# A two-layer encoder trunk on one core: the norm's last squares summed in PSUM, products pinned behind the norm, state tables in fewer transfers

## The chip, the cores and the metric

The kernel runs on one core of one Trainium2 chip. The time is the device time of one execution in microseconds (us); lower is better. The engines are named as in the profile: PE (matrix products), DVE (vector), ACT (scalar), POOL (GpSimd) and SP, whose queue issues nearly all transfers.

## The reference

512 tokens of 1024 features go through two layers, float32 throughout. `u` of the input projection feeds a state-space mixer, `q`, `k`, `v` a windowed attention.

```
for i in range(2):
    x = x + 0.5 * swiglu(rms_norm(x, ffn1_norm[i]), w_gate, w_up, w_down)
    h = rms_norm(x, mix_norm[i])
    q, k, v, u = split(h @ w_in[i])
    attn = banded_attention(q, k, v, sink, bias)
    ssm = s5_mixer(u, ...)
    x = x + concat(rms_norm(attn), rms_norm(ssm)) @ w_out[i]
    x = x + 0.5 * swiglu(rms_norm(x, ffn2_norm[i]), w_gate, w_up, w_down)
return rms_norm(x, final_norm)

rms_norm: x * rsqrt(mean(x*x) + eps) * g
swiglu:   (silu(x @ w_gate) * (x @ w_up)) @ w_down
```

## The kernel before

`x` is kept transposed in SBUF: eight tiles (k0 to k7) of 128 features x 512 tokens. Every product is made of three matmuls of 128x512 (`mm3`, L214 to L218): weight and activation are split into a high part and a low part (the remainder), and PE adds high x high (L216), high x low (L217) and low x high (L218). The text calls each of these matmuls a product. Weights come in chunks of 128x2048 through two raw buffers on SP's queue (L185); ACT casts the high part (L199) and DVE, sometimes POOL, subtracts for the low part (L202).

The norm is taken apart. `h`'s high part is x times the gain (ACT, L277), the low part follows on DVE (`x_lo`, L283); the factor R = rsqrt(mean(x*x) + eps) of each token is multiplied in after the products. So the products with h can start before R is known. R's way is: ACT squares each tile (`x_sq`, L288), POOL adds the squares tile by tile into the first one (`x_acc`, L295; the last add of an FFN or mixer end is DVE's), PE sums over the partitions by products with a column of ones (`rstd_a`, L325), DVE computes the root on four columns (L328 to L334), PE transposes it out to all partitions (`rstd_b`, L341) and ACT copies it to SBUF (L344). A norm stands ahead of each FFN and each mixer.

`ffn` (L349) works through three groups of hidden tiles; for each hidden tile f it makes a gate and an up product over k0 to k7 (48 matmuls), and after a group the down products. In the first hidden tile of an FFN, the program writes gate k0 to k6, the sums, up k0 to k6, the transposes, then both k7. The mixer's first two u projections (`part`, L783) have the same pattern.

In `mixer` (L755) the work is cut into steps that a table, `ORDER` (L42 to L46), puts in turn: `pu`, `k`, `v`, `q` are projections, `ui` reads u back from DRAM in another layout (it is written there by `u_out`, L772, and read by eight transfers, L778), `l` (`s_load`) and `L` (`s_load2`) load the state tables of a quarter of the groups from DRAM (ed and tb at L806 and L808; fd and td at L815 and L818), `si` (`s_in`, products L830, DVE L835 to L840) and `sc` (`s_scan`, L849 to L862) are the state's way in and its scans, `so` (`s_out`, L879) its way out, `as`, `an`, `ao` the attention. The state tables are computed in the FFN before, as a background task (`set_bg`, `drain`).

The order on each engine is not the program's order. A scheduler that simulates the program decides when each engine issues what, within the data's dependences; buffers in SBUF are slots of 128x512, taken by `slot` and given back by `free`, four to a block, sixteen blocks. It is this scheduler that mixes gate and up products at an FFN's start.

Of the kernel before, what the change touches and what calls it, by code (L numbers as in the profile page):

```python
# [42 lines left out]
l0 ui0 pu2 pu3 ui2 ui1 si0 k l1 ui3 v vt q0 si1 sc0 sc1 l2 q1 si2 l3 L0 q2 si3 q3 sc2 L1 so0 L2 as0 sc3 L3 an0  # L43
# [32 lines left out]
class Emit:  # L76
    def __init__(self, nc, tc, I, out, sb, psum, dram):
# [20 lines left out]
        self.bg = None  # L98

# [219 lines left out]
    def rstd_a(self, acc, n, w=T):  # L319
# [4 lines left out]
        for j in range(c):  # L324
            self.T.matmul(b[:, j:j + 1], acc[:, j * P:(j + 1) * P], self.ones, start=True, stop=True)  # L325
# [11 lines left out]
    def rstd_b(self, s, w=T):  # L337

        b = self.bank()
        for j in range(w // P):  # L340
            self.T.transpose(b[:, j * P:(j + 1) * P], s[:, 4 + j:5 + j].to_broadcast([P, P]), self.ident)  # L341
# [7 lines left out]
    def ffn(self, st, after, tail=None):  # L349
# [3 lines left out]
        for f0, nf in FGROUPS:  # L353
            act = []
            for f in range(f0, f0 + nf):
# [391 lines left out]

    def proj(self, w, m, h, bank):
# [6 lines left out]
    def mixer(self, l, st, after):  # L755
# [34 lines left out]
        dg = self.rstd_a(st["sq"][0], D)  # L790
        part(pu[1], 1, range(KD - 1))
        R = self.rstd_b(dg)
        self.free(st["sq"][0])
        part(pu[0], 0, (KD - 1,))
        part(pu[1], 1, (KD - 1,))
# [4 lines left out]
        tabs, Y = {}, {}  # L800

        def s_load(q):
            E, tt = [[self.slot(), self.slot()] for _ in range(2)], [self.slot() for _ in range(3)]
            for r in range(2):
                for j in range(2):
                    SP.dma_start(out=E[r][j], in_=ed[q, :, r, j * T:(j + 1) * T])  # L806
            for r in range(3):
                SP.dma_start(out=tt[r], in_=tb[q, :, r])  # L808
            tabs[q] = [E, tt]

        def s_load2(q):
            F, TT = [[self.slot(), self.slot()] for _ in range(2)], [self.slot(), self.slot()]
# [547 lines left out]
```

## Time and profile before

| what | before |
|---|---|
| median of 3 runs | 1927.52 us (1925.55 to 1928.21) |
| profiled execution, its own time | 1926.47 us |
| its span in the trace | 1924.7 us |
| PE busy | 1865.4 us, 97% |
| DVE busy | 1123.4 us, 58% |
| POOL busy | 714.8 us, 37% |
| ACT busy | 626.5 us, 33% |
| granted PE clock, mean | 0.984 |

All times inside the run count from the span's start. The program starts at 0, the first mixer's first product stands at 387.79, the second FFN of layer 0 starts at 593.28, the first FFN of layer 1 at 963.95 and its second FFN at 1543.30. A wait is put down to the one that came last. PEclk is the share of full speed that the PE clock was granted, 1.00 for 2.4 GHz, 0.50 for 1.2 GHz; a number between is a mean over a stretch.

### The profile page before, as it was taken

The page shows a single profiled execution, that of the slowest core. Times are in us where ns is not written, and L with a number is a line of the kernel's source. Part 1 is how long each engine was busy: PE and PEld are TensorE (multiplying, and loading weights), DVE is VectorE, ACT ScalarE, POOL GpSimd, SP SyncE. Part 2 cuts the span into 40 slices and gives each one's busy share as a digit, 9 for nine tenths or more (in the row PEclk, how much of TensorE's full clock was granted, in tenths as well). Part 3 has the DMA queues.
Part 4 walks back from the last instruction along what each step waited for, and adds up shares of the span by engine and source line. Part 5 has one row for each costly group of instructions (what it writes and reads, how often), then busy time and mean ns, then how long its engine had stood idle before and what let it go on. Part 6 is the DMA issues. An engine that isn't in the chain of part 4 may idle for free. (4 is left out here: it accounts for less than half of the span.)

```text
span 1924.7 us, 23787 instructions
## 1 busy us (share of the span) xinstructions
PE 1865.4 (97%) x9416; PEld 1510.5 (78%) x9416; DVE 1123.4 (58%) x1713; ACT 626.5 (33%) x954; POOL 714.8 (37%) x596
## 2 busy tenths in 40 slices
PE   8999999997998999999999999999989999999997
PEld 6888888886767888888878888888766678888886
DVE  8646545569888635355674453436697673434435
ACT  5223223322733323223332222224236342222223
POOL 2049899237233015093483351103452230201102
PEclk9999999998899999999999999999989999999998
DMA  5533434576011223233333234424640122222321
GB/s 202 165 121 123 160 125 156 160 244 229 31 67 61 98 104 121 99 131 115 108 134 114 99 133 129 137 98 142 232 171 23 65 79 98 88 107 82 107 97 46
DMA packets 86232, 231.12 MB, mean 120 GB/s; under 512 B 31160, under 2 KB 38504, under 8 KB 70376
## 3 DMA queue, kind: packets, MB, share of 16 engines
q1 hardware_dynamic: 84888, 228.51, 35.0%
q8 instruction: 74, 1.21, 0.3%
q10 hardware_dynamic: 1232, 1.09, 0.2%
q14 instruction: 38, 0.31, 0.0%
HBM read 201.11 MB, written 34.75 MB: 123 GB/s over the span
## 5 line engine op out<-in xcount | busy, mean ns | idle before, releaser
L216 PE MATMUL psum<-blk,whi 128*128 128x512 f32 (+1 forms) x2446 | 954.4, 393 | 9.7 <-ACT blk L277 6.4
L217 PE MATMUL psum<-blk,whi 128*128 128x512 f32 (+1 forms) x2446 | 953.7, 390 | 8.2 <-DVE blk L283 8.2
L218 PE MATMUL psum<-blk,wlo 128*128 128x512 f32 (+1 forms) x2446 | 952.0, 390 | 1.4 <-DVE wlo L202 0.9
L216 PEld LDWEIGHTS psum<-blk,whi 128*128 128x128 f32 x2446 | 462.0, 189 | 108.6 <-ACT blk L277 6.9
L217 PEld LDWEIGHTS psum<-blk,whi 128*128 128x128 f32 x2446 | 461.2, 189 | 106.3 <-DVE blk L283 12.9
L218 PEld LDWEIGHTS psum<-blk,wlo 128*128 128x128 f32 x2446 | 461.2, 189 | 97.9 <-DVE wlo L202 2.0
L199 ACT CAST whi<-raw 128x1024 fp32r<-128x1024 f32 (+1 forms) x310 | 303.4, 1027 | 683.3 <-PE psum L217 476.1
L202 DVE TENSOR_TENSOR wlo<-raw,whi 128x1024 fp32r<-128x1024 f32 (+1 forms) x288 | 419.2, 1490 | 40.6 <-ACT whi L199 30.7
L381 DVE TENSOR_TENSOR blk<-psum,blk 128x512 f32<-128x512 f32 x88 | 60.6, 691 | 343.7 <-PE psum L218 340.2
L407 POOL TENSOR_TENSOR xtile<-xtile,blk 128x512 f32<-128x512 f32 x64 | 88.1, 1378 | 374.3 <-DVE blk L405 370.1
L405 DVE SCALAR_TENSOR_TENSOR blk<-psum,blk 128x512 f32<-128x512 f32 x94 | 64.9, 690 | 214.9 <-PE psum L218 208.9
L380 ACT ACTIVATE blk<-blk 128x512 f32<-128x512 f32 x88 | 55.4, 632 | 301.9 <-DVE blk L378 297.4
L694 POOL TENSOR_TENSOR blk<-blk,blk 128x512 f32<-128x512 f32 x64 | 86.8, 1367 | 92.5 <-PE psum L707 51.7
L378 DVE TENSOR_TENSOR blk<-psum,blk 128x512 f32<-128x512 f32 x88 | 60.2, 688 | 85.7 <-PE psum L218 85.2
L295 POOL TENSOR_TENSOR blk<-blk,blk 128x512 f32<-128x512 f32 x30 | 45.6, 1518 | 155.1 <-ACT blk L288 154.3
L202 POOL TENSOR_TENSOR wlo<-raw,whi 128x1024 fp32r<-128x1024 f32 x22 | 60.4, 2752 | 110.2 <-ACT whi L199 110.0
L695 POOL TENSOR_TENSOR blk<-blk,blk 128x512 f32<-128x512 f32 x64 | 88.1, 1378 | 29.3 <-PE psum L707 14.4
L697 POOL TENSOR_TENSOR blk<-blk,blk 128x512 f32<-128x512 f32 x49 | 77.7, 1590 | 2.4
L385 DVE TENSOR_TENSOR blk<-blk,blk 128x512 fp32r<-128x512 f32 x88 | 76.4, 870 | 0.7 <-ACT blk L384 0.7
L283 DVE SCALAR_TENSOR_TENSOR blk<-xtile,consts,blk 128x512 fp32r<-128x512 f32 x48 | 58.7, 1239 | 10.6 <-ACT blk L277 10.6
L1068 POOL TENSOR_TENSOR xtile<-xtile,blk 128x512 f32<-128x512 f32 x24 | 33.7, 1425 | 72.8 <-DVE blk L1066 68.1
L295 POOL TENSOR_TENSOR blk<-blk 128x512 f32<-128x512 f32 x12 | 19.1, 1595 | 99.4 <-ACT blk L288 99.2
(227 smaller groups left out, 1343.0 us busy)
## 6 DMA issues: line engine op xcount, KB each, us to landing
raw<-w SPq DMA_DIRECT2D x123, 1024.0 KB, 4.8
raw<-w SPq DMA_DIRECT2D x32, 896.0 KB, 4.5
fd<-blk SPq DMA_DIRECT2D x32, 256.0 KB, 2.7
ed<-blk SPq DMA_DIRECT2D x32, 256.0 KB, 3.4
blk<-ed SPq DMA_DIRECT2D x32, 256.0 KB, 5.9
blk<-fd SPq DMA_DIRECT2D x32, 256.0 KB, 4.3
tb<-blk SPq DMA_DIRECT2D x12, 512.0 KB, 2.9
blk<-tb SPq DMA_DIRECT2D x24, 256.0 KB, 6.3
```

Of the source, the lines that this page charges most:

```text
L199: self.S.copy(hi[:, c], raw[:, c])
L202: eng.tensor_tensor(out=lo[:, c], in0=raw[:, c], in1=hi[:, c].bitcast(F32), op=ALU.subtract)
L216: t.matmul(out, wh, xh, start=start, stop=False)
L217: t.matmul(out, wh, xl, start=False, stop=False)
L218: t.matmul(out, wl, xh, start=False, stop=stop)
L295: eng.tensor_tensor(out=acc, in0=acc, in1=sq, op=ALU.add)
L385: V.tensor_tensor(out=lo.bitcast(F32R), in0=s, in1=hi, op=ALU.subtract)
L405: V.scalar_tensor_tensor(t, ps, 0.5, R, op0=ALU.mult, op1=ALU.mult)
L407: (V if last else self.G).tensor_tensor(out=self.x[d], in0=self.x[d], in1=t, op=ALU.add)
L694: Gp.tensor_tensor(out=full(o), in0=mat(a), in1=pwo(w, 0), op=M)
L695: Gp.tensor_tensor(out=full(t), in0=mat(b), in1=pwo(w, 1), op=M)
L697: Gp.tensor_tensor(out=o, in0=o, in1=t, op=sg)
```

## The change

1. `x_acc` no longer adds the squares of the last tile (k7). `rstd_a` takes a list of tiles, and PE adds them in PSUM: two matmuls per column of 128 tokens instead of one. This holds for the four FFN starts and the two mixers; the other norms pass a list of one.
2. `issue_after` keeps the instructions emitted in its block behind a given one in their engine's queue: the up products k0 to k6 behind the sums, both k7 products behind the transposes; in the mixer in the same way with the second u tile.
3. A table is loaded in as few transfers as it has parts, into neighbouring slots: ed in 2 of 128x1024 instead of 4 of 128x512, tb in 1 of 128x1536 instead of 3, fd in 2 instead of 4, td in 1 instead of 2. That is 6 transfers instead of 13 for each of four quarters in two layers, 56 fewer in all, with the same bytes.
4. The first quarter's ed and tb of each layer are issued in the first FFN (`early`, after the background task is drained). `ORDER` loses `l0` and is changed in its first half: `L0` stands behind `q3` now, `sc0` ahead of `v`. Half of the transfers that read u tiles 0 and 1 are issued by ACT.

```diff
 ORDER = """
-l0 ui0 pu2 pu3 ui2 ui1 si0 k l1 ui3 v vt q0 si1 sc0 sc1 l2 q1 si2 l3 L0 q2 si3 q3 sc2 L1 so0 L2 as0 sc3 L3 an0
+ui0 ui1 l1 pu2 pu3 ui2 si0 k ui3 sc0 v vt si1 q0 sc1 l2 q1 si2 l3 q2 si3 q3 L0 sc2 L1 so0 L2 as0 sc3 L3 an0
...
     def x_acc(self, d, st, eng):
-        if d:
-            acc, sq = st["sq"][0], st["sq"][d]
+        if 0 < d < KD - 1 or d and st["h"] is None:
+            acc, sq = st["sq"][0], st["sq"].pop(1)
             eng.tensor_tensor(out=acc, in0=acc, in1=sq, op=ALU.add)
             self.free(sq)
...
         for j in range(c):
-            self.T.matmul(b[:, j:j + 1], acc[:, j * P:(j + 1) * P], self.ones, start=True, stop=True)
+            for i, acc in enumerate(accs):
+                mm = self.T.matmul(b[:, j:j + 1], acc[:, j * P:(j + 1) * P], self.ones, start=i == 0, stop=i == len(accs) - 1)
+        self.rstd_mm = mm
...
                 if f == 0:
                     mm(pg, 0, range(KD - 1))
-                    dg = self.rstd_a(st["sq"][0], D)
-                    mm(pu, 1, range(KD - 1))
+                    dg = self.rstd_a(st["sq"], D)
+                    with self.tc.issue_after(self.rstd_mm.ins):
+                        mm(pu, 1, range(KD - 1))
                     R = self.rstd_b(dg)
-                    self.free(st["sq"][0])
-                    mm(pg, 0, (KD - 1,))
-                    mm(pu, 1, (KD - 1,))
+                    self.free(*st["sq"])
+                    with self.tc.issue_after(self.rstd_mm.ins):
+                        mm(pg, 0, (KD - 1,))
+                        mm(pu, 1, (KD - 1,))
...
+                if last and dp == 1 and early is not None:
+                    early()
...
+    def s_load(self, l, q):
+        ed, _, _, tb = self.s5d[l]
+        E, tt = [self.slot(2), self.slot(2)], self.slot(3)
+        for r in range(2):
+            self.SP.dma_start(out=E[r], in_=ed[q, :, r])
+        self.SP.dma_start(out=tt, in_=tb[q].rearrange("p r c -> p (r c)"))
+        return [E, self.parts(tt, 3)]
...
-                SP.dma_start(out=U[m][j * 16:(j + 1) * 16].rearrange("h (g c) -> h g c", c=NC), in_=src[j])
+                (S if j % 2 and m < 2 else SP).dma_start(out=U[m][j * 16:(j + 1) * 16].rearrange("h (g c) -> h g c", c=NC), in_=src[j])
...
-        dg = self.rstd_a(st["sq"][0], D)
-        part(pu[1], 1, range(KD - 1))
+        dg = self.rstd_a(st["sq"], D)
+        with self.tc.issue_after(self.rstd_mm.ins):
+            part(pu[1], 1, range(KD - 1))
...
+        def s_load2(q):
+            F, TT = [self.slot(2), self.slot(2)], self.slot(2)
             for r in range(2):
-                for j in range(2):
-                    SP.dma_start(out=F[r][j], in_=fd[q, :, r, j * T:(j + 1) * T])
-            for j in range(2):
-                g = q * 8 + j * 4
-                SP.dma_start(out=TT[j].rearrange("p (g c) -> p g c", c=P), in_=td[:, g:g + 4])
+                SP.dma_start(out=F[r], in_=fd[q, :, r])
+            SP.dma_start(out=TT.rearrange("p (g c) -> p g c", c=P), in_=td[:, q * 8:q * 8 + 8])
...
+        def early():
+            e.drain()
+            e.pre = {0: e.s_load(l, 0)}
+
+        e.ffn(st, e.after(s2), early=early)
```

PE at the start of the program, around the sums, before (blk_83 and blk_97 are the high parts of h's tiles k0 to k3 and k4 to k7, blk_84 and blk_98 their low parts, whi_70 and wlo_71 the first hidden tile's weights, whi_135 the second's, blk_109 the squares):

```order
L218 MATMUL psum<-blk_97,wlo_71 128x512
L217 MATMUL psum<-blk_98,whi_70 128x512
L218 MATMUL psum<-blk_97,wlo_71 128x512
L216 MATMUL psum<-blk_83,whi_135 128x512
L217 MATMUL psum<-blk_84,whi_135 128x512
L216 MATMUL psum<-blk_83,whi_135 128x512
L217 MATMUL psum<-blk_84,whi_135 128x512
L325 MATMUL psum<-consts,blk_109 128x1 x4
L218 MATMUL psum<-blk_83,wlo_136 128x512
```

The same place in the change (its lines count one to three more: L217 to L219 are the products, L327 the sums; blk_126 holds the squares of k7):

```order
L217 MATMUL psum<-blk_97,whi_70 128x512
L218 MATMUL psum<-blk_98,whi_70 128x512
L219 MATMUL psum<-blk_97,wlo_71 128x512
L327 MATMUL psum<-consts,blk_109 128x1
L327 MATMUL psum<-consts,blk_126 128x1
L327 MATMUL psum<-consts,blk_109 128x1
L327 MATMUL psum<-consts,blk_126 128x1
...
L217 MATMUL psum<-blk_83,whi_70 128x512
L218 MATMUL psum<-blk_84,whi_70 128x512
L219 MATMUL psum<-blk_83,wlo_71 128x512
```

Before, all 48 products of the first hidden tile and four of the second stand ahead of the sums; now the 21 gate products k0 to k6 do, and the up products follow the eight sums. The same happens at the two second FFNs, where the new order has 59 or 60 products ahead of the sums, most of them of the second hidden tile.

SP's queue at the first mixer, before, from the weights that end the FFN on (ud is u in DRAM, raw the weights):

```order
L806 DMA blk_3115<-ed_417 128x512 x2
L806 DMA blk_2989<-ed_417 128x512
L806 DMA blk_3161<-ed_417 128x512 x2
L808 DMA blk_3161<-tb_420 128x512 x2
L808 DMA blk_3162<-tb_420 128x512 x2
L815 DMA blk_3389<-fd_418 128x512
L806 DMA blk_2990<-ed_417 128x512 x3
L808 DMA blk_2990<-tb_420 128x512
L185 DMA raw_2913<-w 128x2048
L818 DMA blk_3389<-td_419 128x512
L808 DMA blk_2991<-tb_420 128x512 x2
```

And in the change (L760, L761 are `s_load`, L796 and L802 u's write and read):

```order
L760 DMA blk_2713<-ed_418 128x1024 x2
L761 DMA blk_2714<-tb_421 128x1536
L186 DMA raw_2705<-w 128x2048
L186 DMA raw_2779<-w 128x2048
L186 DMA raw_2844<-w 128x2048
L760 DMA blk_3008<-ed_418 128x1024 x2
L761 DMA blk_3009<-tb_421 128x1536
L186 DMA raw_2910<-w 128x2048
L796 DMA ud_2902<-blk_2984 128x512
L796 DMA ud_2902<-blk_2987 128x512
L802 DMA blk_2714<-ud_2902 16x8x64 x4
L802 DMA blk_126<-ud_2902 16x8x64 x4
```

The first quarter's table stands three weight chunks earlier, the second quarter's is the only one that is loaded ahead of u, and u's first two tiles are written and read next; before, 17 table transfers of 128x512 stand in the rows shown.

ACT's queue at the same place in the change, where before no transfer stands:

```order
L348 COPY blk_2903<-psum 128x512
L200 CAST whi_3013<-raw_2844 128x1024 x2
L802 DMA blk_2714<-ud_2902 16x8x64 x4
L802 DMA blk_126<-ud_2902 16x8x64 x4
L200 CAST whi_3120<-raw_2910 128x1024 x2
```

The copy of R (L344 before, L348 now) stood behind the two casts of the chunk whi_3013 (whi_3007 before) and now stands ahead of them; the eight transfers stand ahead of the casts of the first query weights.

## Rows read from the trace of the kernel before

**Rows 1.** The page's first part: busy time, share, instructions.

```profile
PE 1865.4 (97%) x9416; PEld 1510.5 (78%) x9416; DVE 1123.4 (58%) x1713; ACT 626.5 (33%) x954; POOL 714.8 (37%) x596
```

**Rows 2.** Timeline of PE, FFN2 of layer 1: start, us, instruction, count, idle before.

```profile
1540.81 0.39 PE L217 MATMUL psum<-blk,whi 128*128 128x512 f32 x1
...
1543.30 0.62 PE L216 MATMUL psum<-blk,whi 128*128 128x512 f32 x2
...
1549.42 0.50 PE L217 MATMUL psum<-blk,whi 128*128 128x512 f32 x1 [1.42 <-DVE blk L283]
...
1555.06 0.50 PE L218 MATMUL psum<-blk,wlo 128*128 128x512 f32 x1 [0.69 <-DVE wlo L202]
```

**Rows 3.** Waits of PE, 387:490 and 1338:1441: us in total, times, longest.

```profile
PE psum L830 <- DMA blk<-ed: 5.2, 4, 2.8
...
PE psum L830 <- DMA blk<-ed: 7.6, 4, 3.6
```

**Rows 4.** Windows: stretch, length, busy of PE, PEld, DVE, ACT, POOL, PEclk, DMA.

```profile
10.00:20.00 10.00, 8.65 (x33) 5.65 (x33) 9.65 (x8) 8.63 (x15) 8.93 (x6) 1.00 0.70 233
...
593.00:604.00 11.00, 5.88 (x25) 4.23 (x25) 11.00 (x13) 6.54 (x10) 10.69 (x10) 1.00 0.00 1
604.00:608.00 4.00, 3.82 (x10) 2.56 (x11) 4.00 (x11) 1.24 (x2) 0.92 (x1) 0.57 0.00 0
...
1373.00:1439.00 66.00, 54.03 (x477) 43.59 (x477) 61.88 (x83) 16.54 (x30) 44.80 (x27) 0.87 0.63 213
423.00:487.00 64.00, 53.28 (x448) 42.64 (x448) 60.01 (x80) 15.29 (x25) 44.42 (x26) 0.85 0.65 211
```

**Rows 5.** Timeline of PE at the start of the program.

```profile
19.81 0.50 PE L217 MATMUL psum<-blk,whi 128*128 128x512 f32 x1 [0.28 <-DVE blk L283]
...
23.48 0.95 PE L325 MATMUL psum<-consts,blk 128*128 128x1 f32 x8
24.30 0.48 PE L218 MATMUL psum<-blk,wlo 128*128 128x512 f32 x1
```

**Rows 6.** Timelines of PE and DVE in the mixer of layer 0.

```profile
396.86 0.95 PE L325 MATMUL psum<-consts,blk 128*128 128x1 f32 x8
...
406.09 3.24 DVE L769 TENSOR_TENSOR blk<-psum,blk 128x512 f32<-128x512 f32 x3 [3.02 <-ACT blk L344]
...
418.32 2.08 PE L830 MATMUL psum<-blk,blk 128*64 128x64 f32 x64
...
486.59 0.69 DVE L856 TENSOR_TENSOR blk<-blk,blk 64x512 f32<-64x512 f32 x1
```

**Rows 7.** Timeline of PE, FFN2 of layer 0.

```profile
603.84 0.50 PE L217 MATMUL psum<-blk,whi 128*128 128x512 f32 x1 [3.99 <-DVE blk L283]
...
604.43 0.63 PE L217 MATMUL psum<-blk,whi 128*128 128x512 f32 x1
604.86 0.63 PE L218 MATMUL psum<-blk,wlo 128*128 128x512 f32 x1
```

**Rows 8.** Timeline of PE, FFN1 of layer 1, at the sums.

```profile
974.42 1.05 PE L325 MATMUL psum<-consts,blk 128*128 128x1 f32 x8 [0.56 <-DVE blk L295]
```

**Rows 9.** Waits of SP's queue, 395:470: us in total, times, longest.

```profile
SPq L815 <- POOL blk L856: 8.6, 2, 4.5
...
SPq L806 <- POOL blk L856: 3.9, 1, 3.9
```

**Rows 10.** The page's transfers: queue, count, KB each, median us to landing.

```profile
blk<-ed SPq DMA_DIRECT2D x32, 256.0 KB, 5.9
...
blk<-tb SPq DMA_DIRECT2D x24, 256.0 KB, 6.3
...
ud<-blk SPq DMA_DIRECT2D x8, 256.0 KB, 2.2
blk<-ud SPq DMA_DIRECT2D x64, 32.0 KB, 1.9
```

More of the change, by code (lines that the diff above doesn't have):

```diff
@@ L98, in __init__ @@
         self.bg = None
+        self.pre = {}
     def slot(self, n=1, r=False):
@@ L317, in after, with rstd_a @@
         return f
-    def rstd_a(self, acc, n, w=T):
+    def rstd_a(self, accs, n, w=T):
         V = self.V
@@ L340, in rstd_b @@
         for j in range(w // P):
-            self.T.transpose(b[:, j * P:(j + 1) * P], s[:, 4 + j:5 + j].to_broadcast([P, P]), self.ident)
+            mm = self.T.transpose(b[:, j * P:(j + 1) * P], s[:, 4 + j:5 + j].to_broadcast([P, P]), self.ident)
+        self.rstd_mm = mm
         self.free(s)
@@ L346, in rstd_b, with ffn @@
         return R
-    def ffn(self, st, after, tail=None):
+    def ffn(self, st, after, tail=None, early=None):
         V, S = self.V, self.S
@@ L745, in s5_steps, with parts @@
         self.free(Cr, Ci, pe, pf, bb, pad, ks)
+    def s_load(self, l, q):
[5 more added lines that the diff above has]
+        return [E, self.parts(tt, 3)]
+    def parts(self, t, n):
+        i, s, _, _ = self.where.pop(id(t))
+        vs = [t[:, j * T:(j + 1) * T] for j in range(n)]
+        for j, v in enumerate(vs):
+            self.where[id(v)] = (i, s + j, 1, v)
+        return vs
     def proj(self, w, m, h, bank):
@@ L789, in mixer @@
         part(pu[0], 0, range(KD - 1))
-        dg = self.rstd_a(st["sq"][0], D)
-        part(pu[1], 1, range(KD - 1))
+        dg = self.rstd_a(st["sq"], D)
+        with self.tc.issue_after(self.rstd_mm.ins):
+            part(pu[1], 1, range(KD - 1))
         R = self.rstd_b(dg)
-        self.free(st["sq"][0])
-        part(pu[0], 0, (KD - 1,))
-        part(pu[1], 1, (KD - 1,))
+        self.free(*st["sq"])
+        with self.tc.issue_after(self.rstd_mm.ins):
+            part(pu[0], 0, (KD - 1,))
+            part(pu[1], 1, (KD - 1,))
         u_out(0, pu[0])
         u_out(1, pu[1])
-        tabs, Y = {}, {}
+        tabs, Y = self.pre, {}
         def s_load(q):
-            E, tt = [[self.slot(), self.slot()] for _ in range(2)], [self.slot() for _ in range(3)]
+            tabs[q] = self.s_load(l, q)
+        def s_load2(q):
+            F, TT = [self.slot(2), self.slot(2)], self.slot(2)
             for r in range(2):
-                for j in range(2):
[L806 to L812, printed above, removed]
-            for r in range(2):
-                for j in range(2):
-                    SP.dma_start(out=F[r][j], in_=fd[q, :, r, j * T:(j + 1) * T])
-            for j in range(2):
-                g = q * 8 + j * 4
-                SP.dma_start(out=TT[j].rearrange("p (g c) -> p g c", c=P), in_=td[:, g:g + 4])
+                SP.dma_start(out=F[r], in_=fd[q, :, r])
+            SP.dma_start(out=TT.rearrange("p (g c) -> p g c", c=P), in_=td[:, q * 8:q * 8 + 8])
             tabs[q] += [F, TT]
@@ L829, in s_in @@
                         u = U[q][:, g * NC:(g + 1) * NC]
-                        TE.matmul(b[a:a + 64, g * NC:(g + 1) * NC], E[r][g // 4][:, g % 4 * P + a:g % 4 * P + a + 64],
+                        TE.matmul(b[a:a + 64, g * NC:(g + 1) * NC], E[r][:, g * P + a:g * P + a + 64],
                                   u[:, ::-1] if a else u, start=True, stop=True, tile_position=(0, a))
                 v.append(b)
-            self.free(*E[0], *E[1])
+            self.free(*E)
             s = [self.slot() for _ in range(4)]
@@ L1206, in f @@
             add(1, 1, V)
-            dg = self.rstd_a(acc[:, H:T], D, H)
+            dg = self.rstd_a([acc[:, H:T]], D, H)
             store(0, Rn)
@@ L1330, in plan_all @@
         s2 = new_st(gl + GC_MIX)
-        e.ffn(st, e.after(s2))
-        e.drain()
+        def early():
+            e.drain()
+            e.pre = {0: e.s_load(l, 0)}
+        e.ffn(st, e.after(s2), early=early)
         s3 = new_st(gl + GC_FFN2)
```

12 lines of the change are left out of this document (6 added, 6 removed).

## The prediction

> **What bounds the kernel now.** I read the page's busy times first. PE is busy for 97% of the span [rows 1], so any PE idle time is worth something, and any work added to PE is paid in full. One product of 128x512 costs 0.226 us: eleven start between 1540.81 and 1543.30 [rows 2]. The change touches six places: the start of the program, the three later FFN starts and the two mixers. So I read where PE waits there. In the mixers the waits view names one of the state tables (blk<-ed) first: 5.2 us in layer 0 and 7.6 us in layer 1, in four waits each [rows 3]. The windows show a second loss there: PEclk is 0.85 and 0.87 in the scan stretches, so PE runs part of them at the lower of its two levels (1.2 instead of 2.4 GHz) [rows 4]. The same rows show DVE busy for 60.01 of 64 us and 61.88 of 66 us. So a table wait on PE lies beside a DVE that is nearly full, and only part of it is worth anything.
>
> **The six longer sums.** Six norms now send the last tile's squares to PSUM with a second matmul per column: 8 more records on PE each. In the trace 8 records take 0.82 us (23.48 to 24.30) [rows 5]. So each is +0.8 us, +4.9 us over six; each place below holds its own. The adds that go away are on POOL and DVE and were only on the path in one place, below. The Trainium skill ("TensorE: Matmul & The Clock Gate", section "Wait — 56ns, not 53.3ns?") says that start-to-start of a small matmul never drops below about 25 ns. These rows show about 100 ns, so the row is used. With 25 ns, an estimate from that page, the six sums would cost 1.2 us and the forecast would be 3.7 us lower.
>
> **The start of the program.** Before, PE mixes gate and up products as tiles become ready and has 52 products and the sums done at 24.30 [rows 5]. Now only the gate half may run ahead of the sums. Its k6 product waits for DVE's low half at 19.81 [rows 5], the two products left end at 20.3, sixteen records take 1.6 us (21.9), and 31 products follow to reach 52 (7.0 us, 28.9). That is **+4.6 us**, the sum included. From 10 to 20 us PE was busy for 8.65 us at full clock [rows 4]; now it would be about 3.2 us (14 products). What such a gap does is seen at 593 to 604 us: PE busy 5.88 of 11, and the next stretch is granted 0.57 [rows 4], with 0.43 us per product [rows 7]. One such fall costs 4 x 0.43 = 1.7 us. Part of it would lie in waits for DVE, so I take half: **+0.9 us** (ends 0 and 1.7).
>
> **The second FFN of layer 1.** Before, 20 products run between 1543.30 and the wait that ends at 1549.42 [rows 2], gate and up in turn. Now only ten gate products can run until k3's low half lands at 1549.42, ten fewer than before. Later the new order uses products of the next tile as fill; these need their weights' low half, which lands at 1555.06 [rows 2]. Walking the new order with these times, 11 products fewer are done at 1558.5: 2.5 us, with the sum 3.3 us, and half of a clock fall 0.9: **+4.2 us** (ends 1 and 7).
>
> **The second FFN of layer 0.** Here PE waits 3.99 us for the low half of k3 [rows 7]. The new order has two DVE instructions between k4's and k3's low half instead of five, which can take off at most that wait, but leaves PE ten products to do meanwhile instead of 22. Half the wait less, 2.0 us, against 12 products less, 2.7 us, and the longer sum, less a little that is filled behind it: I take **+1.0 us** (ends -3 and +4), the clock fall that is already there included.
>
> **The first FFN of layer 1.** The sum waits 0.56 us for the last add, L295 [rows 8]; that wait goes with the add, and 0.8 us come: **+0.2 us**.
>
> **The mixers.** Three things, for layer 0:
> - The first state products (L830) start at 418.32 [rows 6]. In the new order 112 products stand ahead of them in the mixer instead of 128: 16 x 0.226 = 3.6 us, less the sum's 0.8, so 2.8 us sooner. This needs u sooner too. Before, the sums come at 396.86 and DVE's first u product runs at 406.09, once R is there [rows 6]; 71 of the mixer's products stand ahead of R's transposes, and now 56, so R is 15 x 0.226 - 0.8 = 2.6 us sooner. Table 0 is there from the FFN. The eight u transfers on ACT's queue hold the cast behind them until u has landed in DRAM, 2.2 us [rows 10]. It serves the first query weights, whose products stand some 80 products (18 us) further on, which covers it; without that cover its lateness, 2 to 4 us, would be PE's.
> - DVE's 4.0 idle us of the scan stretch [rows 4] can go if the tables are always there, for PE would then give it work in time. More than that can't go without moving DVE work behind the scans. Ends 0 and 4.0; I take 4.0, since the table waits alone are longer than that [rows 3].
> - With waits shorter, a stretch at 1.2 GHz may go, worth 1.7 us as above; I take half, 0.8 us (ends 0 and 9.6, all the clock that is lost over 64 us at 0.85).
>
> That is 2.8 + 4.0 + 0.8 = **-7.6 us** for each mixer, the longer sum included, -15.2 us for two. Layer 1 has the same pattern, with longer table waits [rows 3].
>
> Fewer transfers as such I cost at nothing: the bytes are the same, 56 issues fewer, and SP has time. Nor is SP at its limit in issuing: its long waits there are for POOL's L856 to give slots back [rows 9].
>
> **The sum.** 4.6 + 0.9 + 4.2 + 1.0 + 0.2 = +10.9, less 15.2: -4.3 us against the profiled execution's 1926.47 us, so 1922.2. That execution lies 1.05 us under the median of the runs, 1927.52, so the forecast for the median is **1923.2 us**. A measurement here can tell about 0.2%, 3.9 us, from no change. With m for what one mixer saves, the time is 1938.4 - 2m: faster by over 0.2% when m is above 7.4, slower by over 0.2% when m is below 3.5.
>
> **Rivals.**
> - *Slots, not issues, hold the tables* (slower). A table load now needs two or three neighbouring slots at once, so it waits for the last of them. SP's waits speak for it: 8.6 us for L856 at the second-half tables and 3.9 us at the first [rows 9], and tables take 5.9 and 6.3 us to land where the u rows, of 32 KB, take 1.9 [rows 10]. The Trainium skill ("DMA: Bandwidth & Descriptors", "Issuing engines are not separate DMA queues") says that issuing from several engines saves only issue time, as all run on the same 16 DMA engines. By that rule ACT's half of u brings nothing either. Then only the earlier first products remain: m = 2.8, and 1932.8 us. It decides below m = 3.5. Against it: the first table is loaded before the mixer and needs none of this. Chance 0.25.
> - *DVE hides the tables* (same). Nothing in [rows 4] says that DVE's 4.0 idle us are waits for tables; if only half are, and the clock stays as it is, m is 2.8 + 2.0 = 4.8: 1928.8 us. Chance 0.28.
> - *The tables were the bound* (much faster). All table waits and the lost clock go: m near 15, 1908 us. Against it: DVE's 4.0 us [rows 4]; DVE work would have to move behind the scans, as attention's could. Chance 0.08.
> - *The pins do not bite*: if the low halves come earlier than I walk, the +10.9 shrinks to some 5, with m as forecast: 1917 us. Chance 0.06.
>
> My forecast itself has 0.33 and is the likeliest. Faster is then 0.33 + 0.08 + 0.06 = 0.47, same 0.28, slower 0.25; the forecast lies near the bound of same. The range goes from the much faster case, 1908, to the slot case, 1933, with a microsecond on either side: **1907 to 1934**.
>
> **What the profile after would show.** Right at the start: L327 records from about 20.3 to 21.9 and 52 products done near 28.9; wrong if PE has them before 27. Right in FFN2 of layer 1: a PE wait of 3 to 4 us on L284 that ends with k3's low half. Right in the mixers: no PE wait on blk<-ed over 1 us, DVE without gaps from the first scan on, the way from the first state products to the end of the last scan's L873 (L856 before) about 65 us instead of 69.0 (418.32 to 487.28 [rows 6]), and a PEclk above 0.88 there. The slot case would show SP waiting at the tables for slots and the same waits on PE under other lines. The forecast is wrong if the FFN starts cost nothing, or if the mixers' length changes by less than 4 or more than 12 us.

## The result, and the profile after

The change made the kernel **slower**: 1948.64 us (median of 4 runs, 1947.86 to 1952.69) against 1927.87 us for the kernel before beside it (4 runs, 1925.55 to 1931.39). The ratio is 1.0104, with a 95% interval from 1.0090 to 1.0119. The forecast was 1923.2 us and its range ended at 1934. The profiled execution of after took 1952.69 us, 4 us over its own median. What set that execution apart from the others was not found.

The page's first part, after, to be read beside [rows 1]:

```profile
span 1950.9 us, 23766 instructions
...
PE 1879.7 (96%) x9464; PEld 1521.5 (78%) x9464; DVE 1117.5 (57%) x1708; ACT 626.7 (32%) x954; POOL 720.0 (37%) x595
```

PE has 48 records more, as forecast, and is busy for 14 us longer, which 48 small records don't explain: products at 1.2 GHz are longer. (A float32 matmul of one column stands in the trace as two records, so the eight matmuls of a longer sum are sixteen records.) The rest of the 26 us is waiting. To find the places I matched PE's products in both traces by the order of the program and cut the span at the first product of each stage. What a stretch took after, less what it took before, in us:

| stretch (before) | start of program (34.82) | mixer 0, u to GLU (109.85) | mixer 0, GLU to FFN2 (95.63) | FFN2 of layer 0, start (30.71) | FFN1 of layer 1, start (26.46) | mixer 1, u to GLU (109.09) | mixer 1, GLU to FFN2 (95.57) | FFN2 of layer 1, start (26.84) |
|---|---|---|---|---|---|---|---|---|
| forecast | +5.5 | -7.6 | with it | +1.0 | +0.2 | -7.6 | with it | +4.2 |
| measured | +9.05 | +3.17 | +3.95 | +5.38 | +4.06 | -0.50 | -2.49 | +4.57 |

A start is the way from the first product of an FFN to the first of its third hidden tile; at the start of the program it counts from 0. The eight sum to +27.2; the four stretches left sum to -1.0, the largest -0.73. The four starts cost 23.1 us, all forecast but too small; the mixers should have paid for them and cost 4.1 us instead.

PE's timeline at the **start of the program**, after (start, us, instruction, count, idle before), beside [rows 5]:

```profile
19.81 0.80 PE L218 MATMUL psum<-blk,whi 128*128 128x512 f32 x1 [0.70 <-DVE blk L284]
20.83 3.41 PE L327 MATMUL psum<-consts,blk 128*128 128x1 f32 x16
24.10 0.77 PE L217 MATMUL psum<-blk,whi 128*128 128x512 f32 x1
...
28.86 0.40 PE L219 MATMUL psum<-blk,wlo 128*128 128x512 f32 x1
...
33.42 0.60 PE L344 MATMUL psum<-consts,blk 128*128 128x128 f32 x4
```

The sums come where the forecast put them (20.83 for 20.3 to 21.9), but sixteen of them take 3.3 us instead of 1.6, and eleven products after them take 0.43 us each. Only from 28.86 on does one cost 0.23 us, and 52 products are done at 33.4, where 28.9 was forecast and 24.3 was measured before. So PE ran at 1.2 GHz while it waited for gate tiles, and for 9 us after the last of these waits (19.81).

PE's timeline at **FFN2 of layer 0**, after, beside [rows 7]:

```profile
609.98 0.39 PE L217 MATMUL psum<-blk,whi 128*128 128x512 f32 x1
613.29 0.79 PE L218 MATMUL psum<-blk,whi 128*128 128x512 f32 x1 [2.92 <-DVE blk L284]
...
616.38 0.79 PE L218 MATMUL psum<-blk,whi 128*128 128x512 f32 x1 [1.44 <-DVE blk L284]
...
621.10 0.80 PE L218 MATMUL psum<-blk,whi 128*128 128x512 f32 x1 [3.08 <-DVE blk L284]
```

Before, there were two waits for low halves, 1.14 us for k2's and 3.99 us for k3's. Now there are three, for k1's, k2's and k3's, and the granted clock is 0.50 from 612.44 to 626.09, 13.65 us; before it was 3.42 us (604.36 to 607.78). FFN2 of layer 1 has two such waits, 0.73 us for k2's and 2.41 us for k3's. Why k1's low half (L284) comes late in layer 0 is seen on DVE and POOL:

```profile
607.73 1.28 DVE L642 TENSOR_TENSOR blk<-blk 128x32 f32<-128x32 f32 x1
608.93 1.32 DVE L643 TENSOR_TENSOR blk<-blk 128x32 f32<-128x32 f32 x1
...
612.50 0.73 DVE L284 SCALAR_TENSOR_TENSOR blk<-xtile,consts,blk 128x512 fp32r<-128x512 f32 x1
```

```profile
603.45 6.76 POOL L1085 TENSOR_TENSOR xtile<-xtile,blk 128x512 f32<-128x512 f32 x5 [18.14 <-DVE blk L1083]
```

L642 and L643 belong to the background task, 32 columns wide. An instruction of that width and kind took 0.18 us at 600.61, with POOL idle. Beside POOL's additions it takes 1.3 us: five of them (L642, L643, L634, L635, L638) stand ahead of the low halves for which PE waits, and hold them up by some 5.5 us in all (an estimate, their times less 0.18 us each). Before, such instructions took 1.25 us there too, but PE then had gate and up products to fill with.

PE at the sums of **FFN1 of layer 1**, after, beside [rows 8], and behind it DVE there:

```profile
990.78 1.72 PE L327 MATMUL psum<-consts,blk 128*128 128x1 f32 x14
...
1000.52 0.65 PE L344 MATMUL psum<-consts,blk 128*128 128x128 f32 x4 [2.87 <-DVE blk L337]
```

```profile
994.05 0.15 DVE L331 TENSOR_SCALAR blk<-psum 128x4 f32<-128x4 f32 x1
994.23 0.89 DVE L333 TENSOR_SCALAR blk<-blk 128x4 int32<-128x4 int32 x1
995.15 1.02 DVE L335 SCALAR_TENSOR_TENSOR blk<-blk 128x4 f32<-128x4 f32 x1
996.21 0.16 DVE L336 TENSOR_TENSOR blk<-blk 128x4 f32<-128x4 f32 x1
996.40 1.14 DVE L337 SCALAR_TENSOR_TENSOR blk<-blk 128x4 f32<-128x4 f32 x1
...
997.77 0.95 DVE L336 TENSOR_TENSOR blk<-blk 128x4 f32<-128x4 f32 x1
...
998.95 1.11 DVE L335 SCALAR_TENSOR_TENSOR blk<-blk 128x4 f32<-128x4 f32 x1
...
1000.30 0.16 DVE L337 SCALAR_TENSOR_TENSOR blk<-blk 128x4 f32<-128x4 f32 x1
```

The wait for the last add is gone, as forecast. But the transposes now stand right behind the up products, and these run out 2.87 us before the root is ready. Every second or third instruction of the root, four columns wide, takes about 1 us instead of 0.16. POOL, which works on the next state tables meanwhile:

```profile
997.60 1.10 POOL L703 TENSOR_TENSOR blk<-blk,blk 128x512 f32<-128x512 f32 x1
998.78 1.26 POOL L705 TENSOR_TENSOR blk<-blk,blk 128x512 f32<-128x512 f32 x1
```

Each of the five long instructions ends within 0.04 us of the end of one of POOL's (997.77 + 0.95 beside 997.60 + 1.10, 998.95 + 1.11 beside 998.78 + 1.26). So it looks as if they were held until POOL's instruction ends, and not slowed.

PE's waits in the **mixers**, after: 396:500 for layer 0, behind it 1364:1470 for layer 1 (us in total, times, longest), beside [rows 3]:

```profile
PE psum L896 <- POOL blk L873: 6.0, 2, 4.7
PE psum L982 <- DVE blk L948: 4.3, 1, 4.3
PE psum L896 <- DMA blk<-td: 3.3, 1, 3.3
```

```profile
PE psum L847 <- DMA blk<-ed: 5.5, 1, 5.5
PE psum L982 <- DVE blk L948: 4.9, 1, 4.9
PE psum L896 <- POOL blk L873: 2.0, 1, 2.0
```

In layer 0 the wait for ed is gone; in layer 1 one of 5.5 us is still there (7.6 in four before). In its place, in layer 0, PE waits for the scans' last step on POOL (L873), for a query tile of the attention on DVE (L948), and for td. The windows, after, from the start of the first scan to the end of the last, layer 0 and layer 1 (length, busy of PE, PEld, DVE, ACT, POOL, PEclk, DMA):

```profile
429.34:494.33 64.99, 48.63 (x413) 38.92 (x413) 59.49 (x74) 14.64 (x21) 47.66 (x27) 0.83 0.58 204
1396.64:1461.40 64.76, 51.04 (x447) 41.24 (x445) 59.28 (x74) 16.42 (x24) 47.60 (x27) 0.84 0.61 209
```

And the same of before, where [rows 4] give a stretch cut to whole microseconds:

```profile
422.88:487.28 64.40, 53.68 (x451) 43.00 (x451) 60.41 (x80) 15.57 (x26) 44.54 (x26) 0.85 0.65 210
1373.51:1438.67 65.16, 53.24 (x470) 42.89 (x468) 61.74 (x82) 16.21 (x29) 44.28 (x26) 0.87 0.64 216
```

The scans take as long as before, 65.0 us for 64.4 and 64.8 for 65.2. DVE's idle time grew from 4.0 to 5.5 us in layer 0 and from 3.4 to 5.5 in layer 1, POOL has 3 us more, the granted clock fell a little, and PE did 38 and 23 records fewer meanwhile. These are not products of 128x512; of those it did 14 and 13 more, which stood ahead of the scans before. Fewer are the small records: of the state's way out (`s_out`, L879 before, L896 now) 88 for 130 and 120 for 148, of the attention's scores 12 and 14 for 18, of the turn of the state's output 0 for 4. In layer 0, in these windows before and after (records, busy us, mean ns, idle time before them and what ended it; four more of L879 have a row of their own):

```profile
L879 PE MATMUL psum<-blk,blk 128*64 128x128 f32 x126 | 12.7, 365 | 1.7 <-DMA blk<-fd 1.7
```

```profile
L896 PE MATMUL psum<-blk,blk 128*64 128x128 f32 x88 | 9.8, 400 | 10.8 <-POOL blk L873 6.0 <-DMA blk<-td 3.3 <-DVE blk L985 1.4
```

By their distances at 2.4 GHz elsewhere in the trace of before (0.055, 0.32 and 0.12 us) I estimate these records at 4.7 and 3.3 us, which are left for later. In layer 0 the way from the last scan's end to FFN2 grew from 106.0 to 115.0 us: besides that work PE idles 0.8 us more there, and its clock is 0.96 for 0.98, worth some 2.5 us, which makes 8.0 of the 9.0. In layer 1 that way stayed (104.6 and 104.3), since PE idles 2.2 us less there and no longer falls to 1.2 GHz (3.4 us before).

### The profile page after: what moved, and what is told of

It is laid out like the page before. It is cut to its first block, busy times and chain, and to the rows that moved or that the text cites. A ratio compares the mean times of both kernels' runs of the same rounds, so it can differ in the third digit from the quotient of the medians.

```text
span 1950.9 us, 23766 instructions
## 1 busy us (share of the span) xinstructions
PE 1879.7 (96%) x9464; PEld 1521.5 (78%) x9464; DVE 1117.5 (57%) x1708; ACT 626.7 (32%) x954; POOL 720.0 (37%) x595
## 4 chain that ended last, share of the span: by engine, by line
PE 87%; DVE 8%; issue 2%; POOL 1%; DMA 1%; ACT 0%; DVEq 0%; SPq 0%; POOLq 0%; ACTq 0%
PE psum L217 27%; PE psum L218 27%; PE psum L219 27%; PE psum L1030 1%; PE psum L1015 1%; PE psum L896 1%; DVE wlo L203 1%; DVE blk L284 1%; PE psum L983 1%; PE psum L733 1%; DVE blk L866 1%; PE psum L327 1%; PE psum L982 1%; DVE blk L948 1%; PE psum L715 0%
## 5 line engine op out<-in xcount | busy, mean ns | idle before, releaser
L217 PE MATMUL psum<-blk,whi 128*128 128x512 f32 (+1 forms) x2446 | 959.5, 394 | 8.5 <-ACT blk L278 6.4
L219 PE MATMUL psum<-blk,wlo 128*128 128x512 f32 (+1 forms) x2446 | 954.3, 391 | 0.0
L217 PEld LDWEIGHTS psum<-blk,whi 128*128 128x128 f32 x2446 | 463.4, 190 | 107.5 <-ACT blk L278 6.7
L219 PEld LDWEIGHTS psum<-blk,wlo 128*128 128x128 f32 x2446 | 463.2, 189 | 95.5 <-DVE wlo L203 0.4
L284 DVE SCALAR_TENSOR_TENSOR blk<-xtile,consts,blk 128x512 fp32r<-128x512 f32 x48 | 56.2, 1187 | 10.9 <-ACT blk L278 10.9
L390 ACT CAST blk<-blk 128x512 fp32r<-128x512 f32 x88 | 54.0, 614 | 5.2 <-DVE blk L387 5.2
```

The costliest lines, as they stand in the source:

```text
L217: t.matmul(out, wh, xh, start=start, stop=False)
L219: t.matmul(out, wl, xh, start=False, stop=stop)
L284: self.V.scalar_tensor_tensor(lo.bitcast(F32R), self.x[d], self.gains[:, st["g"] + d:st["g"] + d + 1], hi, op0=ALU.mult, op1=ALU.subtract)
```

## The experiments

Each kernel went through the same scheduler. The expectations name a theory by the part of the change that it blames: the pins, the longer sums, the tables, PE's clock, the root, the slots. The table gives the ratio to before with its 95% interval, the median in us, and for the profiled execution the difference to before by stretch, as above (FFN starts; both parts of a mixer together):

| kernel | median | ratio | start | FFN2 L0 | FFN1 L1 | FFN2 L1 | mixer 0 | mixer 1 |
|---|---|---|---|---|---|---|---|---|
| after | 1948.64 | 1.0104 [1.0090, 1.0119] | 9.05 | 5.38 | 4.06 | 4.57 | 7.1 | -3.0 |
| a1_sums | 1944.32 | 1.0073 [1.0052, 1.0095] | 1.16 | 0.07 | 4.02 | 1.33 | 5.5 | 4.0 |
| a2_sums_pins | 1947.78 | 1.0101 [1.0068, 1.0133] | 8.12 | 5.23 | 4.00 | 5.04 | 2.8 | 2.8 |
| a3_tables | 1932.15 | 1.0013 [1.0003, 1.0022] | 0.65 | 0.85 | 0.01 | 0.05 | 2.4 | 0.6 |
| a4_no_pins | 1954.92 | 1.0123 [1.0103, 1.0142] | 1.18 | 0.94 | 4.05 | 1.38 | 7.8 | 7.7 |
| b1_pins_mixer | 1936.59 | 1.0036 [1.0019, 1.0053] | 0.45 | 0.92 | 4.03 | 1.36 | 5.0 | -2.3 |
| b2_warm | 1954.54 | 1.0131 [1.0101, 1.0161] | 5.59 | 2.13 | 4.00 | 4.13 | 6.3 | -3.0 |
| b3_chain_after | 1952.34 | 1.0121 [1.0102, 1.0139] | 8.56 | 2.21 | 2.45 | 4.16 | 10.9 | -4.3 |
| b4_chain_before | 1922.47 | 0.9967 [0.9952, 0.9982] | 0.51 | 0.33 | 0.03 | 0.00 | -0.8 | -4.9 |
| c1_tables_pinmix | 1931.46 | 1.0008 [0.9997, 1.0019] | 0.05 | -1.59 | -0.01 | 0.06 | 2.3 | 0.9 |
| c2_pinmix | 1930.04 | 1.0005 [0.9991, 1.0018] | 0.78 | 0.41 | 0.03 | 0.06 | 1.5 | -0.3 |
| c3_sums_mix | 1935.25 | 1.0030 [1.0019, 1.0041] | 0.71 | -2.00 | -0.02 | 0.05 | 6.8 | 2.5 |
| c4_narrow | 1932.82 | 1.0018 [1.0007, 1.0029] | 0.58 | -0.33 | 0.01 | 0.01 | -2.7 | 5.4 |
| d1_bg_early | 1955.12 | 1.0130 [1.0114, 1.0145] | 8.90 | 6.77 | -2.39 | 4.12 | 3.7 | 6.7 |
| d2_by_layer | 1929.23 | 0.9995 [0.9987, 1.0004] | 0.57 | 1.22 | 0.03 | 0.03 | -2.6 | 2.6 |

The profile is one execution, so the stretches need not sum to a median's difference (a2_sums_pins was profiled 10 us above its median). b2_warm ran twice, the others 4 to 11 times. With FFN starts as before and no edit near it, FFN2 of layer 0 alone moved by -2.0 to +1.2 us.

### The parts one by one

a1_sums is before with part 1 of the change alone, a2_sums_pins with parts 1 and 2, a3_tables with parts 3 and 4; a4_no_pins is after without its pins:

```diff
-    with self.tc.issue_after(self.rstd_mm.ins):
+    if True:
```

> The kernel before with the last tile's squares summed in PSUM, and nothing else. Theory PINS (the FFN starts lose their time because the products are pinned): only the 48 added sum records cost, about 5 us less a wait of 0.6 us, so 1931 to 1933 us (+0.2 to +0.3%). Rival SUMS (the longer sums themselves, with what they push aside, cost most of the 21 us): 1940 us or more. Rival TABLES (the mixers' new loads and order cost it): as PINS, 1931 to 1933.

> The kernel before with the sums in PSUM and the pins, tables and order of the mixers as before. PINS: the whole loss of the four FFN starts is here, 9 + 5.5 + 4 + 4.3 = 23 us, with the mixers as before or 2 us shorter: 1948 to 1951 us. SUMS: as a1, 1940 or more. TABLES: near a1, 1931 to 1935.

> The kernel before with the wide table loads, the first table issued in the FFN, the new order and ACT's half of u, but the sums as before and no pins. PINS: the FFN starts are as before, and the mixers are about even, +7 and -3 us as in the changed kernel: 1924 to 1933 us. TABLES: 1943 us or more. If the mixers' earlier s_in came from the pins, s_in starts at about 30 us into the mixer again.

> The changed kernel without the pins: sums, tables and order as changed. PINS: 1929 to 1937 us, the four FFN starts back within 1 us of before plus the longer sum. TABLES: 1945 us or more.

The sums alone cost 0.73%, 14 us. At three starts they are near the price forecast, 0.1 to 1.3 us. At FFN1 of layer 1 they cost 4.0 us, and in the mixers 9.5 us. The longest waits of PE in the whole of a1_sums name no sum:

```profile
PE psum L1005 <- DVE blk L997: 8.7, 2, 4.8
PE psum L837 <- DMA blk<-ed: 8.6, 6, 2.2
PE psum L343 <- DVE blk L336: 7.7, 2, 5.0
```

Of these only the attention's (L997) is new. For ed PE waited longer before (12.7 us), and for the root 5.5 us, 5.0 of them at the end of the program then as now; the 2.7 that are new lie at FFN1 of layer 1. So in the mixers other parts of the order came out differently. The pins add 7 us at the start, 5 and 4 us at the second FFNs (a2 less a1). The tables alone bring no gain: 0.13% slower. a3_tables has the wide loads, the early table, the new `ORDER` and ACT's half of u together; c4_narrow below takes out the width, and no run parts the other three. And leaving all pins away does not make after faster: in the profiled execution the starts give back 15.5 us, and the mixers lose 11.4. So a4_no_pins is a miss: *PINS* had 1929 to 1937 us, and though 1954.92 lies where *TABLES* put it, a3_tables has the tables without the loss. By medians a2_sums_pins and a1_sums can't be told apart.

### Pins in the mixers alone, and PE kept at work

b1_pins_mixer is after with that same edit in `ffn` only. b2_warm is after with 24 products more ahead of the program's first sums, into a spare bank that nothing reads, each pinned behind its tile's gate products to fill the waits:

```diff
-    mm(pg, 0, range(KD - 1))
+    for k in range(KD - 1):
+        mm(pg, 0, (k,))
+        with self.tc.issue_after(self.last.ins):
+            for _ in range((0, 0, 2, 9, 3, 10, 0)[k]):
+                self.last = self.T.matmul(wb, wh[:, 0:P], h[0][0].bitcast(F32R), start=True, stop=True)
```

> The changed kernel with the pins in the mixers alone, none at the FFN starts. If the FFN pins cost what their stretches show (8 us at the start of the program, 4.4 and 3.2 us at the two second FFNs, 15.6 in all) and the mixer's pins save: 1931 to 1936 us against 1948.6 for the changed kernel. If the pins are not the cause and the stretches only shift time: 1945 us or more.

> The changed kernel with 24 products more at the start of the program, of k0 into a bank that nobody reads, put where PE waits for the next tile of the gate half. They do no work; they only keep PE busy. CLOCK (half of the loss at the start is PE running at 1.2 GHz through the sums and the up half): products at 0.23 us from about 14 us on, and the third hidden tile's first product at 39 to 41 us instead of 43.9. WAIT (the loss is the wait for the low halves alone): 43.5 to 45 us as before or later.

Without the pins in `ffn` the profiled execution is 17.0 us shorter (1935.66 for 1952.69); 8.6, 4.5 and 3.2 us of it, 16.3, are at the three starts. By medians it is 0.68%, 13 us. So beside the mixers' pins the FFN's pins are most of the loss. The parts don't add up, though: a1_sums has no pin and costs 0.73%, a4_no_pins has none and costs 1.23%. PE's timeline at the start in b1_pins_mixer, where gate and up products are mixed again:

```profile
22.08 1.84 PE L327 MATMUL psum<-consts,blk 128*128 128x1 f32 x16
23.78 0.49 PE L217 MATMUL psum<-blk,whi 128*128 128x512 f32 x1
```

The sixteen sums take 1.7 us, at 2.4 GHz. So they do in b2_warm, which has only the gate products ahead of them, as after has, and idle ones (L378) between:

```profile
18.14 2.43 PE L378 MATMUL psum<-blk,whi 128*128 128x512 f32 x10
20.41 0.39 PE L218 MATMUL psum<-blk,whi 128*128 128x512 f32 x1
...
21.09 1.84 PE L328 MATMUL psum<-consts,blk 128*128 128x1 f32 x16
22.79 0.49 PE L218 MATMUL psum<-blk,whi 128*128 128x512 f32 x1
```

Its start costs 5.6 us instead of 9.05, and its third hidden tile starts at 40.4, where *CLOCK* put it (39 to 41). So at least 3.5 us of the start's price was the clock. The 5.6 us left are the useful work that the pins put off, the longer sum included, and up to 0.6 us by which the idle products themselves hold up the last gate products (20.41 for 19.81). Its time as a whole is not lower; in its profiled execution it lost 6.7 us in the rest of the first FFN, where after lost nothing (one wait there, of 4.8 us, is for POOL's background work). FFN2 of layer 0, with the same pins as after, costs 2.1 us there, so 5.4 is not the pins' price alone; it depends on the order that the scheduler makes there.

### Scan work taken away

b3_chain_after is after, b4_chain_before before, without the backward half of the scans' second combination (that part of the state is left out):

```diff
-                eng.tensor_tensor(out=x[:, :, ::-1], in0=y, in1=z, op=op)
+                if op == B:
+                    eng.tensor_tensor(out=x[:, :, ::-1], in0=y, in1=z, op=op)
```

> The changed kernel with the reversed upper half of the scans' second combination left out (three POOL instructions of 1.7 us and one on DVE of 0.7 us in each mixer; the backward half of that result is not computed). CHAIN (the mixers are bound by the scans' instructions on DVE and POOL, and tables that come sooner change nothing): the last scan ends 3 to 6 us sooner in each mixer, 1937 to 1944 us. TABLES (what bounds is still the loads): within 2 us of 1948.6 us.

> The kernel before with the same part of the scans left out. CHAIN: the table waits of PE lay beside the scans already in the kernel before, so it gains as the changed kernel does, 6 to 11 us: 1917 to 1923 us. TABLES: in the kernel before the table waits are the bound, so it gains under 2 us: 1926 us or more.

From the start of the first scan to the end of the last, the scans took 60.3 and 61.7 us in b4 for 64.4 and 65.2 in before, and the first part of each mixer became 3.0 us shorter, while PE's waits for ed tables in layer 0 stayed (5.5 us in two, for 5.2 [rows 3]). So that part hangs on the scans' chain on DVE and POOL; the table waits lay beside it. b4's 1922.47 us lie in *CHAIN*'s range. In after the scans shrank less, from 65.0 to 63.4 us and from 64.8 to 62.3, and the first parts by 4.5 and 1.3 us. (Counted from DVE's wait ahead of it, before's first scan is 2.4 us earlier; here it counts from its own start.) But layer 0 gave it all back behind the scans (+12.25 where after had +3.95), with a new wait of PE's, 500:616, for the GLU's activations, and b3 came out at 1952.34 us, above after: neither *CHAIN* (1937 to 1944) nor *TABLES* (within 2 us of 1948.6) held.

```profile
PE psum L983 <- ACT blk L1021: 6.9, 1, 6.9
```

### Pins, sums and tables in the mixer

c1_tables_pinmix is a3_tables with the mixer's pins, c2_pinmix is before with the mixer's pins, c3_sums_mix is b1_pins_mixer with the longer sum at the mixers only. c4_narrow is a3_tables with every table in single slots again, 13 transfers, in the new places:

```diff
-        E, tt = [self.slot(2), self.slot(2)], self.slot(3)
+        E, tt = [[self.slot(), self.slot()] for _ in range(2)], [self.slot() for _ in range(3)]
```

> Tables, order and ACT's half of u as changed, pins in the mixers alone, sums as before. If the longer sums cost what b1's stretches show without FFN pins (4 us at the first FFN of layer 1, 1 to 1.4 us at the two second FFNs, 0.5 at the start, 0.8 in each mixer): 1926 to 1930 us. If the sums cost only their records: 1931 to 1934 us.

> The kernel before with the pins in the mixers alone, nothing else. The root and its copy then come about 2.6 us sooner in each mixer, and with them the first scan. CHAIN: the scans start 2 to 3 us sooner and end as much sooner, 1921 to 1926 us. If what PE lacks is work beside the scans: the gain is taken back behind them, 1926 to 1930 us.

> As b1 (pins in the mixers alone, tables as changed), but with the longer sums in the mixers alone; the FFN starts add all eight squares as before. If the wait of 2.9 us at the first FFN of layer 1 comes from the sums that are early there: that stretch is 26.5 us again instead of 30.5, and the whole is 1929 to 1932 us against 1936.6 for b1. If it comes from elsewhere (the shorter background, the mixers): 1934 us or more.

> As a3 (new order, first table in the FFN, ACT's half of u, sums as before, no pins), but each table in 13 transfers again, into single slots. SLOTS (wide loads wait for neighbouring slots, the rival of the prediction): 4 us or more faster than a3's 1.0013. COUNT (fewer issues bring the tables sooner): 4 us or more slower. CHAIN: within 3 us of a3, since neither sets the time.

c1 and c2 can't be told from before; the gain that *CHAIN* gave c2 (1921 to 1926 us) did not come. c3, with the longer sum at the mixers alone, is 0.22% over c1, 4 us, most of it in mixer 0; and without the longer sum the start of FFN1 of layer 1 costs nothing, as its expectation had it, though the whole (1935.25) is above the 1929 to 1932 that stood with it. c4 and a3 differ by 0.05%, less than either's interval: six transfers into neighbouring slots or thirteen into single ones make no difference to the whole. But the mixers of c4 took 202.8 and 210.1 us where those of a3 took 207.9 and 205.3 (before: 205.5 and 204.7).

### The root alone, and the best pieces together

d1_bg_early is after with the next state tables' background work spread over less of the FFN, so that it is done ahead of FFN1 of layer 1. d2_by_layer takes for each layer what had come out short: layer 0 as in c4, layer 1 with wide tables, pins and the longer sum in the mixer; FFN starts as before.

```diff
-            e.set_bg(e.s5_steps(l + 1), 180, 150)
+            e.set_bg(e.s5_steps(l + 1), 180, 85)
```

> The changed kernel with the background task of layer 1's state tables run off in the second FFN of layer 0, so that POOL no longer works on it when the first FFN of layer 1 starts. ROOT (there the root's small DVE instructions take about 1 us instead of 0.16 each because POOL works beside them, and PE waits 2.9 us behind them): they take 0.16 to 0.2 us, the wait goes, and the stretch to the third hidden tile is 27 to 28 us instead of 30.5. ORDER (the transposes are simply queued too early): the wait stays at 2 us or more.

> A kernel put together from the better parts: layer 0's mixer as in c4 (narrow loads, no pins, sums as before: 202.8 us there), layer 1's as in b1 (wide loads, pins, longer sum: 202.4 us), no pins and no longer sums at the FFN starts. If a mixer's length is set by which steps are loaded and pinned: 1922 to 1925 us, 0.2 to 0.3% under the kernel before. If it is set by how the order falls out as a whole: one of the two mixers is 4 us or more longer than there, and the time is 1927 to 1932 us.

DVE at the root in d1_bg_early, with POOL idle beside it:

```profile
1004.84 0.16 DVE L331 TENSOR_SCALAR blk<-psum 128x4 f32<-128x4 f32 x1 [4.45 <-PE psum L327]
...
1006.81 0.16 DVE L337 SCALAR_TENSOR_TENSOR blk<-blk 128x4 f32<-128x4 f32 x1
```

The root takes 2.1 us instead of 6.4 (994.05 to 1000.46 in after), and PE's transposes no longer wait for it. In d1's order 31 products stand between the sums and the transposes, 21 in after; but the root is ready 2.4 us behind the sums, which 21 products, 4.7 us, would have covered too. The start is 6.5 us shorter than after's, with the background's own products gone from it too: with them moved, the stretch ahead is 11.6 us longer and the one behind 11.0 us shorter. As a whole d1 is no faster than after; its mixers cost 10.4 us for after's 4.1.

d2 reproduced layer 0 (202.9 us for c4's 202.8). Layer 1 came out at 207.2 where b1 had 202.4 with the same mixer code, and d2 can't be told from before: a mixer's length is not set by which steps are loaded and pinned alone. No kernel of this study beats before with the whole computation in it; b4, which does, leaves work out.

## Why the prediction was wrong, step by step

The profiled executions differ by +26.2 us where -4.3 was forecast, the medians by +20.8. The stretches below are those of the profiled executions.

- **"-7.6 us for each mixer".** This is the step that failed: +4.1 instead of -15.2, 19.3 of the 30.5 us. Its first term, 2.8 us, came true: in both layers the first state products start 27.8 us into the mixer (30.5 and 30.3 before), the first scan 32.6 us in (35.1 and 34.9), and the last ends at 97.6 and 97.4 (99.5 and 100.0). The second term, 4.0 us, was wrong from the start, and the trace of before showed it. I took DVE's idle time for table waits because these were longer. DVE's own waits in the scans of before (us in total, times, longest) name POOL's add of the state's way in (L839), which stands right behind DVE's own products:

```profile
DVE blk L849 <- POOL blk L839: 2.9, 3, 1.2
DVE blk L931 <- ACT blk L930: 0.7, 1, 0.7
DVE blk L968 <- PE psum L966: 0.5, 1, 0.5
```

  Nor do the tables stand behind these: the state products that had waited 2.8 us for ed were done at 443.3, and DVE, busy till then, took them up at 449.0. In after that wait is still there, and one for PE's projections has come:

```profile
DVE blk L944 <- PE psum L219: 2.9, 1, 2.9
DVE blk L866 <- POOL blk L856: 2.1, 2, 1.7
```

  The third term, half a clock stretch gained, has the wrong sign: 0.83 and 0.84 where above 0.88 was to be seen. So the way from the first state products to the last scan's end is 69.8 us; 65 was forecast, and before had 69.0. What I had no term for is PE's other work. Of the state's way out and the attention's scores less is done beside the scans, 4.7 and 3.3 us by estimate, and layer 0 pays for that behind them. In layer 1 less waiting and a higher clock there make up for it, and the first term alone remains: -3.0.
- **The start, +5.5 us.** The mechanism was right and the size off. The work put off is at most 5.6 us by b2_warm, for 4.6. The clock term was the mis-sized one, at least 3.5 us for 0.9, and outside its ends (0 and 1.7): I priced one fall of four products, and the sixteen records of the sums and eleven products behind the wait ran at 1.2 GHz too. (4 x 0.43 is also the whole time of four slow products and not what the clock adds to them, 0.2 us each. That the sum is near the 1.6 us that the eight products of a fall of 3.42 us lose is chance.)
- **FFN2 of layer 1, +4.2 us.** Right: +4.57, with waits on L284 of 0.73 and 2.41 us where one of 3 to 4 was forecast, and 4.1 to 5.0 in the other kernels with these pins. Its terms were not measured apart; the clock was at 1.2 GHz for 6.8 us there, longer than the half fall that I priced, so how far the terms made up for each other by chance is open.
- **FFN2 of layer 0, +1.0 us.** Above its end of 4: +5.4. The wait for k3's low half, that I hoped to halve, went from 3.99 to 3.08 us only, one of 2.92 us for k1's came, and the three make 7.4 us for 5.1 in two before; the clock stayed low for 13.65 us. I counted the instructions between two low halves and took no account of their length: the background's took 1.3 us each beside POOL. With other orders around it the same pins cost from 2.1 to 6.8 us.
- **FFN1 of layer 1, +0.2 us.** The wait for the add did go. I did not ask what is late next: the root. It was as slow before (instructions of up to 1.14 us), but then 72 products stood ahead of the transposes, for 42 now, and covered all but 0.5 us of it. a1, a4 and b1 show the same 4.0 us with the longer sum and no pin there, c3 none without it.
- **The six longer sums, +0.8 each.** About right at full clock where nothing else moved (1.2 to 1.3 us at the start and at FFN2 of layer 1 in a1). Alone (a1_sums) they cost 14 us, 4.0 of them at FFN1 of layer 1; most of the rest is in the mixers, where the order changed with them.
- **The rivals.** *Slots, not issues, hold the tables* gave 1932.8 us, the only slower one, by a mechanism that c4_narrow refutes. SP's waits at 395:470 in after, those for weights and for reading u left out, speak against it too:

```profile
SPq L796 <- DVE blk L793: 13.1, 3, 11.7
SPq L834 <- PE psum L847: 5.9, 1, 5.9
SPq L761 <- PE psum L847: 2.8, 1, 2.8
SPq L760 <- POOL blk L873: 1.9, 1, 1.9
```

  The three waits at tables are 10.6 us, for 12.5 before [rows 9]; the longest is for u itself. (The mixer starts 8.9 us later in after; behind that window lies one more, 4.4 us at L834. Before, all waits at tables in the window make 23 us.) *The tables were the bound* falls with a3 and b4, *the pins do not bite* with b1. *DVE hides the tables* is right about what bounds the scans, but none of its gain from DVE came either. No rival held the time, because none let the mixers lose while the starts cost more.

What stays open is why an order falls out as it does. The mixers took from 202 to 213 us in the kernels that do the whole work, and no single part of the change accounts for which.

## What to carry to other kernels

A pin that keeps filler work behind a late sum cost twice here: the work put off, and the clock that was low in the gap and stayed low for the work behind it. A wait on a transfer need be no price while a nearly full chain on other engines runs beside it; take a piece out of the chain first, as b4_chain_before did, to see which of the two sets the end. Where a scheduler writes the order, a local edit is also a new order everywhere: run each part by itself, and ask of a removed wait which instruction is late next.

## What the runs showed of the hardware

- An instruction of four columns on DVE took 0.16 us with POOL idle and up to 1.14 us beside POOL's products and adds of 128x512, 1.1 to 1.6 us each; one of 32 columns 0.18 and 1.3 us. The long ones of after, at FFN2 of layer 0 and FFN1 of layer 1, end within 0.06 us of the end of one of POOL's. The Trainium skill ("SBUF — State Buffer", section "Who interferes with whom") says that a DVE instruction with two inputs in SBUF contends with a GpSimd instruction that reads SBUF. The rows of FFN1 of layer 1 agree for L335 to L337. L333, which has one input, took 0.89 us there as well; that sentence is on two inputs, and no run shows why it was held.
- A record of a one-column sum, half of a matmul, took 0.10 to 0.11 us at 2.4 GHz (1.70 us for sixteen in b1_pins_mixer) and 0.20 at 1.2 GHz (3.27 us in after).
- At a program start with waits between its products PE was still at 1.2 GHz at 28 us. With 24 idle products in those waits it was at 2.4 GHz at 17 us (three started in 0.68 us). It is not the same in each execution: a2_sums_pins and b3_chain_after, with the same start, had a PEclk of 1.00 from 10.6 to 16.7 and of 0.50 from 17.4 to 26.9. (For 10 to 28 us of after the windows print 1.00; there the distance of the products, 0.43 us, shows the lower level.)
